# More projection beside the convolution's last stage, less beside its middle stages, and 256 bytes between two pools of a hybrid encoder layer

## The chip, the cores and the metric

The kernel runs on one core of a Trainium2 chip. The core has five engines with an instruction queue each: TensorE (PE, matrix products), VectorE (DVE), ScalarE (ACT), GpSimd (POOL) and SyncE (SP, which here only issues transfers). Transfers between DRAM and the on-chip memory (SBUF, 128 partitions) go through 16 DMA engines. Products land in PSUM, eight banks of 128 x 512 numbers. The metric is the device time of one execution in microseconds, lower is better; the median of three runs stands for a kernel.

## The reference

One layer of a bidirectional encoder on x of 2048 x 1024, all in float32:

```python
u = _rms_norm(h, norm_mix_g[l])
proj = u @ w_in[l]                                   # 1024 -> 3600 columns
hy = _short_conv_centred(proj[..., :HY_COLS], ...)   # 3 x 512 columns: z and two gates
spec = _hyena_filter_spectrum(L, ...)                # long filters, one per order and channel
y_hy = _group_rms_norm(_hyena(hy, spec, hy_skip[l]), hy_norm_g[l], HYENA_GROUPS)
qk = jax.nn.silu(_short_conv_centred(proj[..., HY_COLS:off], ...))
y_ml = _mlstm_bidirectional(q, k, v, o_pre, gates, ml_gate_b[l])
y_ml = _group_rms_norm(y_ml, ml_norm_g[l], MLSTM_HEADS)
h = h + concatenate([y_hy, y_ml]) @ w_out[l]
h = h + _cross_attention(_rms_norm(h, norm_x_g[l]), _rms_norm(mem, norm_mem_g[l]), wq, wk, wv, wo)
h = h + square(relu(_rms_norm(h, norm_ff_g[l]) @ ff_w1[l])) @ ff_w2[l]
return _rms_norm(h, final_norm_g)
```

`_hyena` does, for each of two orders, a convolution over the whole length by an FFT of twice the length, and a multiplication by a gate: `z = gate * (irfft(rfft(z) * spec[:, o]) + z * skip[o])`. `_mlstm_bidirectional` is a recurrence over chunks in both directions. The memory `mem` has 256 rows.

## The kernel before

Every large product is made of three products of operands split into a high and a low part (`mm3`, L353 to L359). The program is written by Python generators, each of which yields a stated cost before a piece of work; two generators are woven by these costs:

```python
def weave(a, b, wa, wb, until=False):
    ...
        if fb or (not fa and da / wa <= db / wb):
                da += next(a)
        else:
                db += next(b)
```

The weave fixes the program order. A planner then places the instructions on the engines' queues by a simulated timeline, with the program order as priority; instructions marked `keep_in_program_order` stay in order among themselves. At run time each queue is worked off in order.

The stretch in question weaves `rest` (the projections) with `p.hyena` (the long convolution) in the proportion 445 to 329 (L2125).

**Projections.** `sweep` (L748) makes transposed tiles, 128 columns by 512 rows, for the columns that need the short convolution; it yields 5.5 for 24 products and is heavy on DVE and ACT besides (short convolution, splits, transposes back). `natural` (L860) makes tiles of 128 rows by 256 columns for v and the gates; it yields 11 for four tiles and needs little of DVE and ACT. Beside them `gates` (L1076) and `states` (L1223, the backward recurrence) are stepped at fixed places. After the weave come the memory's projections `memproj` (L693: L708, L725, L737), with the first five steps of `mlstm` (L1227) between their steps.

**The convolution.** `hyena` (L905) has these stages: `spectrum` for order 0 (8 steps), then for each order 16 middle steps (loads of a block of the spectrum and of the filter, `response` L952, products L1030, element-wise complex product L1032 to L1036 on ACT, DVE and POOL, product back L987, store L989) and 8 last steps (load3, products L1048, gate L1051). For order 0 a last step goes on with `spectrum(1)`; for order 1 it takes squares on POOL (L1060), a sum (L1062), `bank_rsqrt` (L205 to L217) in a PSUM bank, L1064, two products on POOL (L1066) and the stores of `yh` (L1068). The yields that set its pace are 4.6 for a middle step, 6.0 for a last step of order 0 and 4.5 for one of order 1.

**PSUM.** The tags "mm" and "hy" have four banks each, given out in program order. The convolution, the recurrences and attention's transposes all use "hy".

**The mLSTM.** `mlstm` computes decay rows (L1275 to L1293), takes scores in a "hy" bank (L1284), and does 16 chunks one after the other (L1322 to L1356). Its pool `m_sb` lies on the space of the projections' x tiles.

**Attention.** `tail_open` (L1366) opens the pools of what comes next, on the left side of SBUF where the projections' and the convolution's pools were: `t_w` (first pair of weight tiles), `t_acc`, `t` (a pair of activation tiles and the second pair of weight tiles) and `t_n` (four staging tiles "wn" of 2 KB per partition, then two activation tiles). `mixed(0)` (L1484) loads the first four row blocks of `yh` into staging tiles (L1473), turns them on PE (L1479) and splits them; `gemm` then multiplies by the first and second pairs of w_out. Adding up the tiles, the pool `i_sb`, which the projections and `memproj` use (weights, memory tiles, small tiles), ends at byte 88,320 of a partition, and `t_n` begins at byte 88,064.

Of the kernel before, what the change touches and what calls it, by code (L numbers as in the profile page):

```python
# [10 lines left out]
F32 = mybir.dt.float32  # L11
# [117 lines left out]
class Prog:  # L129
# [775 lines left out]
    def hyena(self, es):  # L905
# [19 lines left out]
        def ta():  # L925
            return sb.tile([128, 2, CH], F32, tag="a", name="a", bufs=10)

        def tb():
            return sb.tile([128, CH], F32, tag="b", name="b", bufs=5)
# [12 lines left out]
        def load_filter(o, i):  # L942
            dm = sb.tile([128, 2, 128], F32, tag="dm", name="dm", bufs=3)
            nc.sync.dma_start(out=dm, in_=a["c_dm"][:, 2 * i:2 * i + 2])
            return dm, load_block(fs[o], i)

        def load2(o, i):
            em = sb.tile([128, 2, 128], F32, tag="em", name="em", bufs=2)
            nc.sync.dma_start(out=em, in_=a["c_em"][:, 2 * i:2 * i + 2])
            return em, load_block(sds[o], i)  # L950

        def response(i, dm, t):  # L952
            hr, hi = ta(), ta()
            for m in range(2):
                pp = self.mm()
                nc.tensor.matmul(pp, dm[:, m], t[:, m], start=True, stop=True)
                nc.scalar.copy(hr[0:64, m], pp[0:64])
                nc.scalar.copy(hr[64:128, m], pp[0:64])
                nc.vector.tensor_copy(hi[64:128, m], pp[64:128])
                nc.vector.tensor_copy(hi[0:64, m], pp[64:128])  # L960
                if i == 0 and m == 0:
                    nc.scalar.copy(hr[64:65, 0], pp[64:65])
                    for r in range(2):
                        nc.vector.memset(hi[64 * r:64 * r + 1, 0], 0.0)
            return dm, hr, hi

        def load3(o, j2):
            js = slice(2 * j2, 2 * j2 + 2)
            r = [ta() for h in range(2)]
            for h in range(2):  # L970
                self.by_phase(nc.sync, gds[o], j2, h, r[h], True)
            gate = ta()
            for q in range(4):
                nc.sync.dma_start(out=gate[phase[q]], in_=hy[1 + o, q, :, js])
            return r, gate
# [3 lines left out]
        def late(f):  # L979
            if held:  # L980
                held.pop()()
            if f is not None:
                held.append(f)

        def back(m, i, em, y, gs, dst):
            pg = self.hy()
            nc.tensor.matmul(pg, em[:, m], y, start=True, stop=True)  # L987
            nc.scalar.copy(gs[:, m], pg)
            nc.gpsimd.dma_start(out=of_block(dst, i, m), in_=gs[:, m])  # L989

        def spectrum(o, j2, z):
            st = [ta() for h in range(2)]
            pp = [self.hy() for q in range(4)]
            self.beside(*((pp[q][own[jj]], f1[phase[q]], z[phase[q], jj]) for q in range(4) for jj in range(2)),
                        pin=1 if o else 2)
            for i in range(2):
                for h in range(2):
                    (nc.vector.tensor_copy if h else nc.scalar.copy)(st[h][:, i], pp[2 * h + i])
            for h in range(2):
                self.by_phase(nc.gpsimd, sds[o], j2, h, st[h])  # L1000
# [12 lines left out]
        for o in range(2):  # L1013
            gd = gds[o]
            nxt = load2(o, 0)
            ready = response(0, *fq.pop(0))
            yield 4
            for i in range(16):
                yield 4.6
                dm, hr, hi = ready  # L1020
                em, t = nxt
                if i < 14:
                    fq.append(load_filter(o, i + 2))
                if i < 15:
                    nxt = load2(o, i + 1)
                    ready = response(i + 1, *fq.pop(0))
                gs = ta()
                for m in range(2):
                    pp = self.hy()
                    nc.tensor.matmul(pp, dm[:, m], t[:, m], start=True, stop=True)  # L1030
                    xt, y = tb(), tb()
                    nc.scalar.activation(xt[0:64], pp[64:128], AF.Copy, scale=-1.0)  # L1032
                    nc.scalar.copy(xt[64:128], pp[0:64])
                    nc.vector.tensor_tensor(y, pp, hr[:, m], ALU.mult)
                    nc.gpsimd.tensor_tensor(xt, xt, hi[:, m], ALU.mult)
                    nc.vector.tensor_tensor(y, y, xt, ALU.add)  # L1036
                    late(lambda m=m, i=i, em=em, y=y, gs=gs: back(m, i, em, y, gs, gd))
            late(None)
            nxt = load3(o, 0)
            yield 5  # L1040
            for j2 in range(8):
                yield 4.5 if o else 6.0
                js = slice(2 * j2, 2 * j2 + 2)
                r, gate = nxt
                if j2 < 7:
                    nxt = load3(o, j2 + 1)
                pp = [self.hy() for jj in range(2)]
                self.beside(*((pp[jj][phase[q]], e2[own[jj]], r[q // 2][own[jj], q % 2])  # L1048
                              for jj in range(2) for q in range(4)), pin=True)
                for jj in range(2):  # L1050
                    nc.vector.tensor_tensor(gate[:, jj], pp[jj], gate[:, jj], ALU.mult)  # L1051
                if o == 0:
                    late(lambda j2=j2, gate=gate: spectrum(1, j2, gate))
                    if j2 > 5:
                        fq.append(load_filter(1, j2 - 6))
                    continue
                y = gate.rearrange("q j (g e) -> q (j g) e", g=8)
                sq = ta()
                sqv = sq.rearrange("q j (g e) -> q (j g) e", g=8)
                nc.gpsimd.tensor_tensor(sqv, y, y, ALU.mult)  # L1060
                ms = sb.tile([128, 16], F32, tag="ms", name="ms", bufs=2)
                nc.vector.tensor_reduce(ms, sqv, AX.X, ALU.add)  # L1062
                rv = self.bank_rsqrt(sb, ms, 64)
                nc.vector.tensor_tensor(sqv, y, rv.unsqueeze(2).broadcast_to([128, 16, 64]), ALU.mult)  # L1064
                for jj in range(2):
                    nc.gpsimd.tensor_tensor(sq[:, jj], sq[:, jj], ghy, ALU.mult)  # L1066
                for q in range(4):
                    nc.gpsimd.dma_start(out=yh[q, :, js], in_=sq[phase[q]])  # L1068
            late(None)
# [296 lines left out]
    def tail_open(self, es):  # L1366
        def pool(name):
            return es.enter_context(self.tc.tile_pool(name=name, bufs=1))

        self.wp = [pool("t_w"), None]  # L1370
        for tag in ("wh", "wl"):
            self.wp[0].tile([128, 8, 256], F32R, tag=tag, name=tag)
        self.acc = pool("t_acc").tile([128, 8, 512], F32, name="acc")
        self.wp[1] = self.ap = pool("t")
        self.acts = 2
        for _ in range(2):
            self.act_tile("act")
        for tag in ("wh", "wl"):
            self.wp[1].tile([128, 8, 256], F32R, tag=tag, name=tag)
        self.T = pool("t_n")  # L1380
        self.acts = self.wps = 0

# [819 lines left out]
```

## Time and profile before

| | us |
|---|---|
| three runs | 3058.41, 3061.78, 3063.68 |
| median | 3061.78 |
| the profiled execution | 3063.97 |
| its span, first to last instruction | 3062.3 |

The span is the time from the first to the last instruction of the profiled execution; about 1.7 us lie around it. In the profile a line such as L1284 is a line of the listing above. PE is busy for 97% of the span and DVE for 64%. The mean clock granted to TensorE is 0.989 of full speed. Matmuls are pipelined: a product of 128 x 512 is shown for about 0.39 us, and the next begins 0.23 us after it.

The stages of the stretch, from the order of lines on PE:

| us from the span's start | what PE does |
|---|---|
| 351 to 410 | sweeps; the convolution's `spectrum` for order 0 |
| 408 to 620 | sweeps, then natural tiles; middle steps of order 0 |
| 638 to 735 | natural tiles, sweeps; last steps of order 0 |
| 745 to 955 | sweeps, natural tiles; middle steps of order 1 |
| 966 to 1087 | the last projections, then `memproj` from 997; last steps of order 1 |
| 1104 to 1132 | `memproj`; the first two chunks of the mLSTM |
| 1132 to 1172 | mLSTM chunks and attention's first turns, alone |
| from 1172 | attention woven with the rest of the mLSTM |

### The profile page before, as it was taken

Reading aid. Unit: us, or ns where it says so; the run is one execution under the profiler, and the core shown is the slowest. Engines: PE = TensorE matmul, PEld = TensorE weight load, DVE = VectorE, ACT = ScalarE, POOL = GpSimd, SP = SyncE. Lnnn points to the kernel's source line nnn. Section 1 sums busy time; section 2 is a strip of 40 time slices with the busy share of each in tenths; the row PEclk is TensorE's granted clock in tenths of the full one; section 3 lists DMA queues with packets and bytes.
Section 4 is the critical chain, followed back from the end, with each engine's and each line's share of the span. In section 5 each row is a group of like instructions: output and inputs, shape, how many; then the busy total and the mean of one; then the engine's idle time right before and its main releaser. Section 6 shows DMA issues by size and latency. Waiting matters only on the chain.

```text
span 3062.3 us, 44144 instructions
## 1 busy us (share of the span) xinstructions
PE 2979.0 (97%) x14799; PEld 2367.6 (77%) x14799; DVE 1953.2 (64%) x3442; ACT 1491.5 (49%) x2930; POOL 1263.4 (41%) x1025
## 2 busy tenths in 40 slices
PE   9999999998999989999999999999999999999998
PEld 7666667775678867888888888888888888888876
DVE  8855464557755447867665666558555686566695
ACT  6443455634664235555544455556555543333335
POOL 0112113321443654333223247765665374344653
PEclk9999999999999999999999999999999999999999
DMA  6655676686877976463567466657544555444434
GB/s 223 197 186 170 213 263 214 192 273 216 279 229 221 348 265 198 149 228 125 196 202 264 137 219 217 208 178 250 190 151 152 196 192 169 118 157 121 155 103 165
DMA packets 423644, 607.03 MB, mean 198 GB/s; under 512 B 36847, under 2 KB 229999, under 8 KB 422393
## 3 DMA queue, kind: packets, MB, share of 16 engines
q1 hardware_dynamic: 395972, 525.42, 53.6%
q0 software_dynamic: 18992, 62.96, 5.6%
q10 hardware_dynamic: 8452, 15.83, 1.4%
q8 instruction: 117, 1.92, 0.3%
q14 instruction: 111, 0.90, 0.1%
HBM read 401.67 MB, written 202.41 MB: 197 GB/s over the span
## 4 chain that ended last, share of the span: by engine, by line
PE 58%; DVE 2%; DMA 1%; issue 1%; ACT 1%; POOL 0%; SPq 0%; DVEq 0%; POOLq 0%; ACTq 0%
PE mm L355 12%; PE mm L359 12%; PE mm L358 12%; PE hy L355 6%; PE hy L359 6%; PE hy L358 6%; PE hy L1322 1%; PE hy L1324 1%; DVE bl L1693 0%; PE hy L1284 0%; PE hy L1596 0%; DVE acc L1991 0%; PE hy L1200 0%; PE hy L1479 0%; DVE acc L2028 0%
## 5 line engine op out<-in xcount | busy, mean ns | idle before, releaser
L1692 ACT CAST ah<-w 128x512 fp32r<-128x512 f32 x284 | 176.6, 623 | 303.8 <-PE hy L358 150.2
L1693 DVE TENSOR_TENSOR bl<-wr,bh 128x512 fp32r<-128x512 f32 x213 | 240.3, 1132 | 126.5 <-ACT bh L1692 126.2
L366 DVE TENSOR_TENSOR wl<-wn,wh 128x512 fp32r<-128x512 f32 (+1 forms) x296 | 220.0, 787 | 89.2 <-ACT wh L366 89.2
L355 PE MATMUL mm<-xh,wh 128*128 128x512 f32 x640 | 264.5, 415 | 2.3 <-ACT xh L366 1.1
L358 PE MATMUL mm<-xl,wh 128*128 128x512 f32 x640 | 255.9, 400 | 5.5 <-DVE xl L366 5.4
L359 PE MATMUL mm<-xh,wl 128*128 128x512 f32 x640 | 254.5, 398 | 0.0
L1692 ACT CAST bh<-wr 128x512 fp32r<-128x512 f32 x232 | 143.4, 621 | 227.9 <-PE mm L359 169.5
L1693 DVE TENSOR_TENSOR al<-w,ah 128x512 fp32r<-128x512 f32 x236 | 216.5, 918 | 57.2 <-ACT ah L1692 56.9
L359 PE MATMUL mm<-bh,al 128*128 128x512 f32 x576 | 223.8, 391 | 3.4 <-DVE al L1693 3.4
L355 PE MATMUL mm<-bh,ah 128*128 128x512 f32 x576 | 225.9, 392 | 1.3 <-DVE acc L1854 1.1
L358 PE MATMUL mm<-bl,ah 128*128 128x512 f32 x576 | 224.9, 390 | 0.0
L366 ACT CAST wh<-wn 128x512 fp32r<-128x512 f32 (+1 forms) x296 | 164.3, 620 | 102.6 <-PE mm L359 51.1
L358 PE MATMUL mm<-act,wh 128*128 128x512 f32 x512 | 202.0, 395 | 0.0
L359 PE MATMUL mm<-act,wl 128*128 128x512 f32 x512 | 199.9, 392 | 0.0
L355 PE MATMUL mm<-act,wh 128*128 128x512 f32 x512 | 199.0, 395 | 0.6 <-ACT wh L366 0.5
L355 PE MATMUL hy<-bh,ah 128*128 128x512 f32 x448 | 175.2, 391 | 0.0
L358 PE MATMUL hy<-bl,ah 128*128 128x512 f32 x448 | 174.6, 390 | 0.0
L359 PE MATMUL hy<-bh,al 128*128 128x512 f32 x448 | 174.4, 390 | 0.0
L331 POOL TENSOR_TENSOR b<-b 128x512 f32<-128x512 f32 x32 | 48.1, 1504 | 293.6 <-DVE b L330 277.4
L355 PEld LDWEIGHTS mm<-xh,wh 128*128 128x128 f32 x640 | 121.1, 190 | 52.4 <-issue 18.7
L358 PEld LDWEIGHTS mm<-xl,wh 128*128 128x128 f32 x640 | 121.2, 189 | 50.9 <-issue 19.1
L355 PE MATMUL mm<-wh,xh 128*128 128x256 f32 (+1 forms) x512 | 155.7, 304 | 1.8 <-DVE a L960 1.8
(396 smaller groups left out, 8257.4 us busy)
## 6 DMA issues: line engine op xcount, KB each, us to landing
wr<-hc SPq DMA_DIRECT2D x224, 256.0 KB
w<-in_ff_w_dram SPq DMA_DIRECT2D x172, 256.0 KB
hc<-wn SPq DMA_DIRECT2D x128, 256.0 KB
wn<-in_w_in_dram SPq DMA_DIRECT2D x100, 256.0 KB
hc<-q SPq DMA_DIRECT2D x96, 256.0 KB
fs<-a SPq DMA_DIRECT2D x32, 512.0 KB
zs<-a POOLq DMA_DIRECT2D x32, 512.0 KB, 6.6
a<-fs SPq DMA_DIRECT2D x64, 256.0 KB
```

What stands on the lines that cost most here:

```text
L331: nc.gpsimd.tensor_tensor(b, f, b, ALU.subtract)
L355: first = mm(ps, lh, rh, start=start, stop=False)
L358: mm(ps, lh, rl, start=False, stop=False)
L359: self.last = mm(ps, ll, rh, start=False, stop=stop)
L366: both = (self.nc.scalar.copy(hi, src), self.nc.vector.tensor_tensor(lo, src, hi.bitcast(F32), ALU.subtract))
L1322: nc.tensor.matmul(dst, nm[:, h], va[:, h], start=True, stop=state is None)
L1324: nc.tensor.matmul(dst, rows_[d, 1][:, h], state[:, h], start=False, stop=True)
L1692: self.nc.scalar.copy(hi, src)
L1693: eng.tensor_tensor(lo, src, hi.bitcast(F32), ALU.subtract)
```

## The change

Two yields in `hyena` and one more pool in `tail_open`. The middle steps of both orders state a cost of 3.7 in place of 4.6. The last steps of order 1 state 8.0 in place of 4.5; those of order 0 keep 6.0. A pool of one unused tile of 64 numbers (256 bytes per partition) is opened ahead of `t_n`, so that `t_n`, and with it everything opened later on that side, begins at byte 88,320 in place of 88,064. No instruction is added or removed by the text; the order in which the planner places them is made anew.

```diff
             for i in range(16):
-                yield 4.6
+                yield 3.7
                 dm, hr, hi = ready
...
             for j2 in range(8):
-                yield 4.5 if o else 6.0
+                yield 8.0 if o else 6.0
                 js = slice(2 * j2, 2 * j2 + 2)
...
         for tag in ("wh", "wl"):
             self.wp[1].tile([128, 8, 256], F32R, tag=tag, name=tag)
+        pool("t_even").tile([128, 64], F32, name="t_even")
         self.T = pool("t_n")
```

## The prediction

> **What bounds the kernel now.** I read the page first, then busy time by stage, then what TensorE (PE) waited for in the stages where it was not full.
>
> ```profile
> span 3062.3 us, 44144 instructions
> PE 2979.0 (97%) x14799; PEld 2367.6 (77%) x14799; DVE 1953.2 (64%) x3442; ACT 1491.5 (49%) x2930; POOL 1263.4 (41%) x1025
> ```
>
> PE is busy for 2979.0 of 3062.3 us. The change removes no product, so it can only win or lose in the 83 us of PE idle time, and in the half-speed clock that follows idle time. The windows cut the stretch that the change touches at the convolution's stages: middle stage of order 0, its last stage, middle stage of order 1, its last stage (955 to 1104, in three pieces), and what follows.
>
> ```profile
> core 0: us, PE busy (x) PEld busy (x) DVE busy (x) ACT busy (x) POOL busy (x), PEclk, DMA share, GB/s
> 410.00:640.00 230.00, 223.62 (x1249) 169.17 (x1248) 139.22 (x219) 140.19 (x248) 78.07 (x85) 0.99 0.69 216
> 640.00:735.00 95.00, 84.19 (x548) 57.08 (x554) 55.03 (x169) 31.67 (x53) 9.52 (x17) 0.96 0.82 261
> 735.00:955.00 220.00, 212.57 (x1020) 151.69 (x1006) 144.47 (x249) 135.48 (x236) 87.78 (x97) 1.00 0.73 227
> 955.00:997.00 42.00, 42.00 (x304) 37.21 (x304) 22.20 (x48) 13.84 (x20) 15.56 (x17) 1.00 0.97 303
> 997.00:1050.00 53.00, 50.64 (x266) 42.06 (x273) 23.60 (x77) 17.22 (x43) 36.15 (x44) 0.97 1.04 350
> 1050.00:1104.00 54.00, 54.00 (x262) 37.95 (x247) 24.27 (x68) 12.06 (x23) 33.84 (x39) 1.00 0.98 341
> 1104.00:1132.00 28.00, 28.00 (x145) 19.86 (x144) 13.72 (x38) 14.63 (x50) 16.59 (x19) 1.00 0.69 217
> 1132.00:1172.00 40.00, 23.89 (x139) 21.77 (x138) 27.16 (x101) 22.51 (x86) 18.73 (x18) 0.74 0.59 186
> ```
>
> The last row is the worst: PE is idle for 16.1 of 40 us there, with a granted clock of 0.74. Its waits (engine and line, what it waited for: us, times, longest) are those of a serial chain:
>
> ```profile
> PE hy L1322 <- DVE bry L213: 5.1, 1, 5.1
> PE hy L1479 <- DVE act L366: 5.0, 1, 5.0
> PE hy L1200 <- ACT ht L1336: 2.5, 2, 2.1
> PE hy L1284 <- issue: 1.6, 1, 1.6
> ```
>
> L1284 to L1336 is the mLSTM; L1479 turns attention's first rows of y. Why does the chain stand alone? First and last start of a few lines tell (durations min/median/max, then the starts; L1060 over its first four steps, then over all eight):
>
> ```profile
> L708 PE MATMUL mm<-mt,wm x256: 377/379/483, 997.1 to 1109.6; 128*128 128x256 f32 x128
> L737 PE MATMUL mm<-wm,kt x64: 592/592/595, 1079.2 to 1131.1; 128*128 128x512 f32 x64
> L1293 ACT ACTIVATE rw<-rw,cols x16: 385/386/402, 1001.3 to 1005.7; 128x128 f32<-128x128 f32 x16
> L1284 PE MATMUL hy<-qn,kk_t x48: 272/275/421, 1104.1 to 1169.1; 128*128 128x128 f32 x48
> L1060 POOL TENSOR_TENSOR a<-a x4: 1885/1887/1888, 971.8 to 1035.5; 128x1024 f32<-128x1024 f32 x4
> L1060 POOL TENSOR_TENSOR a<-a x8: 1883/1888/1904, 971.8 to 1093.3; 128x1024 f32<-128x1024 f32 x8
> L1064 DVE TENSOR_TENSOR a<-a,hy x8: 1220/1220/1221, 980.8 to 1101.5; 128x1024 f32<-128x1024 f32 x8
> ```
>
> The memory's products begin with L708 at 997 and end with L737 at about 1131.5 us. The mLSTM's first decay rows were ready at 1006 (L1293), but its first scores (L1284) ran at 1104.1, 1.4 us after the convolution's last L1064 ended (1101.5 + 1.2). The code gives the reason: `scores` takes the next "hy" PSUM bank, and these four banks go round in program order behind the convolution's last `bank_rsqrt`. So the convolution's slow last stage holds the mLSTM back by some 98 us, and of the four chunks written beside the memory's products two run after them with nothing large beside. That is the stall at 1132.
>
> **The change part by part.** The pacer advances projections by 445 for each 329 of the convolution's stated costs. Projection costs are near microseconds: 24 products of 128x512 make 5.5, and 14 steps in this stretch take 52.87 - 49.69 = 3.18 us, 0.227 each, so 24 take 5.45.
>
> ```profile
> 49.69 0.40 PE L355 MATMUL mm<-xh,wh 128*128 128x512 f32 x1
> ...
> 52.87 0.39 PE L359 MATMUL mm<-xh,wl 128*128 128x512 f32 x1
> ```
>
> *Middle steps, 4.6 to 3.7:* each of 32 loses 0.9 x 445/329 = 1.22 us of projection beside it, 39 us in all. *Last steps of order 1, 4.5 to 8.0:* each of 8 gains 4.7 us, 38 us in all. The convolution's total goes from 334.8 to 334.0, so both still run out of cost together; only the last stage begins earlier. Counting the yields, its first step is written when 374 of 451 projection units are out, not 407: 33 us earlier, at about 933 us where it is now 966 (the first L1060 at 939 where it is 971.8).
>
> How fast will its steps go? The rows of L1060 give 63.7 / 3 = 21.2 us a step at first, 57.8 / 4 = 14.5 us for the last four, 17.4 over all. The slow ones lie where the DMA engines are full (shares 0.97 and 1.04), since the memory's weights come in beside the step's own transfers. Begun 33 us earlier, most of the steps precede those weights. At 14.5 the last L1064 starts at 980.8 - 33 + 7 x 14.5 = 1049; at today's 17.2 (120.7 / 7) at 1069. I take 1060: the mLSTM starts about 41 us earlier than now. Another thing it needs, the backward states, had left the core for DRAM by the row below (last store at 1047.4), so they don't hold it later than that.
>
> ```profile
> L1219 POOL DMA_DIRECT2D cbd<-cb x9: 560/580/610, 922.4 to 1047.4; - x9
> ```
>
> 41 us covers the 40 us stretch. What is it worth? 16.1 us of idle time, and the half-speed clock: in the two low pieces below PE is busy for 8.74 + 4.28 = 13.0 us at half, which is 6.5 us lost. At most 22.6 us.
>
> ```profile
> 1140.20:1153.90 13.70, 8.74 (x37) 8.17 (x38) 10.60 (x41) 6.24 (x26) 7.31 (x7) 0.50 0.41 134
> 1164.10:1171.00 6.90, 4.28 (x21) 4.28 (x21) 6.26 (x21) 4.05 (x9) 0.00 (x0) 0.51 0.55 176
> 1020.80:1024.20 3.40, 3.40 (x8) 2.73 (x9) 1.40 (x2) 1.61 (x4) 3.40 (x4) 0.50 1.03 416
> ```
>
> *The 256-byte tile `t_even`:* it adds no instruction. The addresses of the program before put the end of the projections' and the memory's pool at byte 88,320 of a partition, and the staging pool `t_n` at 88,064; its first tile overlaps by 256 bytes. A pool's space is free only when all of its tiles are, and the trace shows that: the queue waited for the memory's last product.
>
> ```profile
> SPq L1473 <- PE mm L737: 1.6, 1, 1.6
> 1131.77 0.81 SPq L1473 DMA_DIRECT2D wn<-yh  x2
> ```
>
> After the change these four loads need only the convolution's end, so they, the 16 turns and the 24 products on the first pair of weights (5.5 us) can stand ready when L737 ends. Queued behind them on SP are the mLSTM's kn, qn and kk_t, which then also stop waiting for L737. What is late next is the second pair of weights, still in the memory's space: nothing if the 5.5 us cover its split, 5 us (the present wait for act) if not. Of the 22.6 us I take 18; bounds 0 and 22.6.
>
> *The stall in the memory's first keys* (row below) and the 3.4 us at half clock behind it are worth 2.4 + 1.7 = 4.1 us. It falls where DMA is full; I take 2, bounds 0 and 4.
>
> ```profile
> PE mm L725 <- ACT kt L710: 2.4, 1, 2.4
> ```
>
> [...]
>
> *The middle stages' lost cover.* Per step PE, DVE and ACT are now busy 212.57, 144.47 and 135.48 / 16 = 13.3, 9.0 and 8.5 us; with 1.2 us less of PE work they still are at 75% or less. Idle time there is 7.4 us, of which:
>
> ```profile
> PE hy L1030 <- DMA a<-zs: 3.2, 1, 3.2
> PE mm L355 <- DVE a L960: 1.8, 1, 1.8
> PE hy L987 <- DVE b L1036: 1.6, 2, 1.3
> ```
>
> The first is the change of order, once. The other 4.2 us lie beside seven steps with transposed projections (sweeps), which load DVE and ACT; by the yields there will be 13 such steps. Six more at 0.6 us cost 3.6; I take 4, bounds 0 and 39 (all the cover lost). The 10.8 us of idle time in 640 to 735 keep their cause (the round trip between orders, and the gates' chain beside it); the gates move to the middle steps of order 1. I take 0, bounds 8 either way, two thirds of what is idle there.
>
> Sum: -18 - 2 + 4 = -16 us. The profiled execution took 3063.97 us, 2.2 above the median; from the median 3061.78 the sum gives **3046 us**.
>
> **The rivals.** *Its own chain paces the last stage.* If all its steps go at 21.2 us, as the first do, the last L1064 starts at 948 + 148 = 1096, 5 us earlier than now, and the stall stays but for that: with the middle stages' 4 us, 3061. The same follows if the planner, which places instructions by its own simulated times, does not put the stage earlier: it lags its written place already (all of it is written ahead of L708, which begins at 997, and it ends at 1103). Against it: the steps speed up as soon as the back states end, and DMA is at 0.73 where the first steps will now lie.
>
> *Slower: the middle stages' latency.* If a middle step cannot go faster than now, because its loads, its DVE and its POOL work follow one another, the 39 us of cover return as PE idle time: 3062 - 20 + 39 = 3081. It decides from 20 us on, 0.6 us for each of 32 steps, half of what is taken away. Against it: PE is 97% busy there, so PE paces the steps now, and their idle time is 13.8 us for 32 steps. For it: the 4.2 us above lie beside the sweeps, and more of the steps are to lie there.
>
> **How the numbers follow.** Forecast 0.60 (own range 3036 to 3056), chain or planner 0.26 (3055 to 3067), slower 0.14 (3064 to 3081). A measurement of this kernel can tell about 0.2%, 6 us, from no change: 3055.7 to 3067.9. Faster: 0.57 of the first and 0.05 of the second, 0.62. Same: 0.03, 0.20 and 0.03, so 0.26. Slower 0.12. The range is 3032 to 3069: it takes in the first two cases, and leaves out 0.1 above and less below (every bound at its best, -35 us, is not to be had at once).
>
> **What would show it.** Right: the last L1060 near 1050, the first L1284 near 1060, loads wn<-yh issued before L737 ends, and the 40 us behind L737 with PE full and the clock at 1. In the middle stages idle time stays below 20 us. Wrong: L1284 still behind 1090; or waits for L1036, L960 or a<-zs that grow; or L1479 and L355 waiting after L737 for the second pair's split.

## The result and the profile after

| | us |
|---|---|
| kernel before, median of 11 runs (lowest to highest) | 3062.72 (3058.41 to 3067.0) |
| kernel after, median of 11 runs (lowest to highest) | 3070.66 (3065.26 to 3074.77) |
| time after / time before | 1.0022, 95% interval 1.0013 to 1.003 |
| the profiled execution after, its span | 3069.03, 3067.3 |

The change makes the kernel slower by 0.22%; 3046 was forecast. The span and the busy times of the page after:

```profile
span 3067.3 us, 44143 instructions
PE 2984.0 (97%) x14799; PEld 2361.9 (77%) x14799; DVE 1944.3 (63%) x3442; ACT 1491.6 (49%) x2930; POOL 1260.5 (41%) x1025
```

TensorE's idle time is the same as before (3067.3 - 2984.0 = 83.3 us, before 3062.3 - 2979.0 = 83.3). It has only moved, as the windows by stage show. First the kernel before, then the one after; the rows are: order 0's middle steps, the change of order (its last steps up to order 1's first middle step), order 1's middle steps, the stretch up to the memory's first product (L708), and 186 us from there, which hold the memory's products and the seam to attention.

```profile
core 0: us, PE busy (x) PEld busy (x) DVE busy (x) ACT busy (x) POOL busy (x), PEclk, DMA share, GB/s
415.00:615.00 200.00, 193.62 (x1024) 143.25 (x1023) 113.61 (x181) 124.17 (x222) 69.29 (x76) 0.98 0.67 211
615.00:754.00 139.00, 124.98 (x810) 90.32 (x810) 89.20 (x229) 55.23 (x97) 22.84 (x32) 0.98 0.82 258
754.00:945.00 191.00, 186.78 (x897) 133.22 (x897) 123.56 (x208) 117.62 (x204) 80.08 (x87) 1.00 0.74 230
945.00:997.00 52.00, 52.00 (x351) 45.00 (x350) 30.35 (x61) 20.88 (x31) 18.19 (x21) 1.00 0.84 261
997.00:1183.00 186.00, 167.53 (x862) 131.22 (x862) 95.86 (x308) 70.63 (x216) 111.60 (x125) 0.94 0.85 284
```

```profile
413.00:597.00 184.00, 173.75 (x848) 121.36 (x847) 108.80 (x168) 117.67 (x209) 67.69 (x76) 0.98 0.71 222
597.00:733.00 136.00, 122.09 (x857) 89.45 (x856) 71.85 (x141) 50.18 (x89) 20.72 (x31) 0.92 0.81 254
733.00:923.00 190.00, 177.56 (x727) 117.03 (x726) 136.94 (x281) 119.66 (x205) 68.11 (x76) 0.96 0.71 213
923.00:1030.00 107.00, 105.33 (x711) 89.72 (x710) 55.85 (x142) 31.37 (x52) 46.79 (x50) 1.00 0.81 248
1030.00:1216.00 186.00, 181.81 (x963) 146.51 (x962) 102.88 (x301) 88.45 (x268) 108.90 (x117) 1.00 0.84 284
```

The last row is the gain: idle time falls from 18.5 to 4.2 us and the clock is full. The second and third rows are the price: in order 1's middle steps idle time rises from 4.2 to 12.4 us, and the granted clock falls to 0.92 at the change of order and to 0.96 behind it. I count as **lost** the idle time of a stretch and half of the time that its clock records show at 0.50 (in the kernel after, products of 128 x 256 begin 0.21 us apart at 0.50, from 883.4 to 886.2, and 0.12 us apart behind it, at full clock):

| lost us | order 0's middle | change of order | order 1's middle | to L708 | memory and seam | sum |
|---|---|---|---|---|---|---|
| before | 9.8 | 17.4 | 4.2 | 0.0 | 30.4 | 61.8 |
| after | 13.7 | 24.0 | 19.4 | 1.7 | 4.2 | 63.0 |

So 26.2 us were won at the seam and 27.4 lost ahead of it. The count serves for large differences only: the span less this sum lies between 2996.9 and 3007.8 us over all the kernels of this study, so it doesn't resolve the last few us (here it shows 1.2 of the 5.0 us between the two spans). It also counts idle time inside a half-clock piece twice. Counted once, as the prediction did at the seam (idle time, and half of PE's busy time at 0.50), 22.5 us were won at the seam (26.7 to 4.2) and 23.9 lost ahead of it (30.9 to 54.8): 4.0, 3.4, 14.8 and 1.7 us by stage. Over the whole spans this second count gives 105.7 and 106.1 us; so 4.6 of the 5.0 us between the two profiled executions lie in neither idle time nor half clock, and where they lie isn't shown.

What TensorE waited for between 410 and 1030 in the kernel after (the six largest; line, what it waited for: us, times, longest):

```profile
PE hy L1030 <- DMA a<-zs: 6.8, 2, 3.9
PE mm L956 <- issue: 5.3, 2, 3.0
PE hy L173 <- DMA a<-zg: 4.4, 2, 2.7
PE mm L956 <- DMA a<-fs: 3.7, 2, 3.4
PE hy L173 <- ACT a L998: 3.0, 1, 3.0
PE mm L956 <- DVE a L960: 2.3, 2, 1.2
```

Three of them are loads from DRAM: of zs and zg, which the stage ahead has stored there, and of fs, the filters' response, stored before this stretch. They come to 14.9 us in all. In the kernel before it was 6.9 us: 3.2 for zs, which the prediction shows, and

```profile
PE hy L173 <- DMA a<-zg: 2.6, 1, 2.6
PE mm L956 <- DMA a<-fs: 1.1, 1, 1.1
```

The starts that the prediction had named (in kernels with `t_even`, lines from 1380 on stand one higher than in the listing), and the issue of the loads of y:

```profile
L1284 PE MATMUL hy<-qn,kk_t x128: 270/275/377, 1093.9 to 1458.8; 128*128 128x128 f32 x128
L737 PE MATMUL mm<-wm,kt x64: 592/592/595, 1117.1 to 1174.0; 128*128 128x512 f32 x64
L708 PE MATMUL mm<-mt,wm x256: 377/379/381, 1030.3 to 1158.8; 128*128 128x256 f32 x128
L1060 POOL TENSOR_TENSOR a<-a x8: 1884/1906/1914, 948.0 to 1087.8; 128x1024 f32<-128x1024 f32 x8
```

```profile
1105.20 1.80 SPq L1474 DMA_DIRECT2D wn<-yh  x4
```

The mLSTM's first scores (L1284) came 10.2 us earlier than before, not 41. But the memory's products were pushed back: L708 begins 33 us later and L737 ends with its last start at 1174.0 in place of 1131.1. The first scores now lie 80 us ahead of the last L737, where it was 27 us, and the loads of y are issued 69 us ahead of it. Both dates, that of the scores and that of the memory's products, come after the time lost ahead of L708: 27.4 us more than before by the count, which is most of L708's 33 us (an estimate) and delays the scores as well. In e4b_last below, which loses about as much ahead as the kernel before (29.9 and 31.4 us), the scores come 31.6 us earlier and L737 ends 12.5 us later. The stall is gone by both moves: the scores come earlier in the work, and the memory's products later.

### The profile page after: what moved, and what is told of

The parts are those of the page before. It is cut to its first block, busy times and chain, and to the rows that moved or that the text cites. A ratio compares the mean times of both kernels' runs of the same rounds, so it can differ in the third digit from the quotient of the medians.

```text
span 3067.3 us, 44143 instructions
## 1 busy us (share of the span) xinstructions
PE 2984.0 (97%) x14799; PEld 2361.9 (77%) x14799; DVE 1944.3 (63%) x3442; ACT 1491.6 (49%) x2930; POOL 1260.5 (41%) x1025
## 4 chain that ended last, share of the span: by engine, by line
PE 80%; DMA 6%; DVE 6%; issue 4%; ACT 2%; POOL 1%; SPq 1%; DVEq 0%; POOLq 0%; ACTq 0%
PE mm L355 17%; PE mm L358 16%; PE mm L359 16%; PE hy L355 6%; PE hy L359 6%; PE hy L358 6%; PE hy L173 2%; PE mm L956 1%; PE mm L708 1%; PE hy L1030 1%; PE hy L987 1%; DMA a<-zg 1%; PE hy L1322 1%; PE hy L1324 1%; PE mm L725 1%
## 5 line engine op out<-in xcount | busy, mean ns | idle before, releaser
L355 PE MATMUL mm<-xh,wh 128*128 128x512 f32 x640 | 265.6, 417 | 4.2 <-ACT st L201 1.4
L355 PE MATMUL mm<-bh,ah 128*128 128x512 f32 x576 | 225.9, 392 | 0.1
L355 PE MATMUL mm<-act,wh 128*128 128x512 f32 x512 | 199.5, 395 | 0.8 <-ACT wh L366 0.8
L355 PE MATMUL hy<-bh,ah 128*128 128x512 f32 x448 | 175.2, 391 | 0.0
L355 PEld LDWEIGHTS mm<-xh,wh 128*128 128x128 f32 x640 | 120.8, 189 | 56.3 <-issue 21.7
L355 PE MATMUL mm<-wh,xh 128*128 128x256 f32 (+1 forms) x512 | 155.0, 303 | 0.8 <-DVE a L960 0.4
```

The costliest lines, as they stand in the source:

```text
L355: first = mm(ps, lh, rh, start=start, stop=False)
```

## The experiments

Theory A at the start: the middle stages' lost cover costs about as much as the seam wins. Its rivals: t_even made the gain (B); any new order of the program moves the time by as much (C); the wide last steps, 8.0, make the loss (D). Every run is a ratio to the kernel before, taken on the same chip in the same set of runs.

### One part at a time

`e1_even` has t_even alone; `e2_yields` the two yields alone; `e3_mid` the 3.7 and t_even; `e4_last` the 8.0 and t_even.

```diff
# e3_mid, against the kernel after
-                yield 8.0 if o else 6.0
+                yield 4.5 if o else 6.0
# e4_last, against the kernel after
-                yield 3.7
+                yield 4.6
```

> The kernel before with t_even alone (yields 4.6 and 4.5). Theory A (less cover in the middle stages costs some 25 us, the early last stage with t_even wins some 22): the loads wn<-yh no longer wait for L737, but the mLSTM chain still stands alone behind L737, since its scores still wait for the last stage's banks; only the 5.0 us of L1479 <- act go: 3058 (3055 to 3062). Theory B (t_even alone made the gain at the seam): 3041 to 3046. Theory C (any rearrangement moves the planner's order by some 8 us, whatever it is): anywhere from 3054 to 3071.

> The kernel after without t_even (yields 3.7 and 8.0). Theory A: the middle stages stay as in the kernel after (3070.7); behind L737 the loads wn<-yh wait again for L737, then 16 turns and a split, but chunks of the mLSTM are later in the program beside them: 3 to 8 us of idle time return at the seam: 3075 (3072 to 3079). Theory B: without t_even nothing of the gain of some 22 us is left: 3090. If t_even is worth nothing: 3070.

> Middle steps 3.7, last steps of order 1 kept at 4.5, with t_even. The middle steps are written as in the kernel after, the last stage begins as early, and its steps stand closer. Theory A: the middle stages' loss of some 25 us is there, with the a<-zs and half-clock pieces at 419, and the gain at the seam too: 3070 (3064 to 3074). Rival D (the loss comes from the last stage's 8.0, its steps spread too far): 3045 to 3052.

> Last steps of order 1 at 8.0, middle steps kept at 4.6, with t_even. Everything to about 960 is written as in the kernel before; the projections run out after four last steps, the other four stand alone in the program ahead of the memory's products. Theory A: middle stages as before (PE idle near 25 us in 410 to 997), the seam as before or a little better: 3059 (3054 to 3066). Rival D (8.0 itself costs): 3070 or more.

| run | ratio (95%) | median us | lost ahead of L708 | lost at memory and seam |
|---|---|---|---|---|
| e1_even | 1.0005 (0.9993 to 1.0017) | 3063.15 | 26.5 | 28.7 |
| e2_yields | 1.004 (1.0025 to 1.0055) | 3071.54 | 56.9 | 9.8 |
| e3_mid | 1.005 (1.0035 to 1.0065) | 3075.15 | 60.0 | 12.3 |
| e4_last | 0.9948 (0.9932 to 0.9965) | 3043.55 | 37.7 | 8.5 |

The last steps at 8.0, with t_even, make the kernel 0.5% *faster*, which I had not expected: theory A had 3059 for it. The middle steps at 3.7, with t_even, make it 0.5% slower. Each of the two edits takes most of the stall at the seam away by itself (30.4 us before; 8.5 and 12.3), and only the middle steps bring the large loss ahead of L708 (31.4 before; 37.7 and 60.0). Rivals B and D fall; of rival C more is said below, where effects add up that a mere reshuffling would scatter.

t_even alone does nothing that can be told from zero. TensorE's two largest waits between 1100 and 1170 in e1_even, and its loads of y:

```profile
PE hy L1322 <- DVE bry L213: 5.1, 1, 5.1
PE hy L1480 <- DVE act L366: 4.8, 1, 4.8
```

```profile
1105.17 1.76 SPq L1474 DMA_DIRECT2D wn<-yh  x4
```

The loads run ahead, at 1105 and not at 1131.77, as the prediction said. But the wait for the split `act` is as long as before (5.0), so it never hung on the loads.

To see what 8.0 does, `e4_last` was run again as `e4b_last`, with its twin without t_even, `e7_last_noeven`.

> The kernel with the last steps alone at 8.0 (middle steps 4.6, t_even) once more, as the measure for the three others of this set: 3044 (3040 to 3048).

> The same without t_even: last steps of order 1 at 8.0 and nothing else of the change. If t_even is what lets attention's first loads run ahead of L737: the loads wait for L737 again and 5 to 6 us come back, as between the kernel after and the one without t_even: 3049 (3046 to 3053). If the seam is gone for another reason (the mLSTM's first chunks lie beside the memory's products): 3044.

Measured: 0.9945 (0.9933 to 0.9958) and 0.9963 (0.9952 to 0.9975), 3041.78 and 3049.24 us. Both as expected: once the chain's stall is gone, the loads of y are late next, and t_even is worth 5.5 us (0.18%); between the kernels after and e2_yields the difference is the same 0.18%. Each of the two is uncertain by nearly as much as it is large; they agree, and the traces below show the wait. The stages of e4b_last (same five windows), and three lines of it:

```profile
413.00:611.00 198.00, 192.79 (x1027) 142.43 (x1026) 113.98 (x181) 124.50 (x222) 69.68 (x76) 0.99 0.67 213
611.00:747.00 136.00, 122.56 (x800) 87.61 (x800) 87.62 (x227) 54.87 (x97) 22.49 (x32) 0.97 0.81 260
747.00:938.00 191.00, 188.04 (x905) 134.53 (x904) 122.77 (x210) 117.78 (x204) 80.01 (x87) 1.00 0.74 233
938.00:999.00 61.00, 57.79 (x392) 48.58 (x391) 35.33 (x87) 20.86 (x32) 26.98 (x32) 1.00 0.86 268
999.00:1185.00 186.00, 180.35 (x958) 142.91 (x957) 108.67 (x321) 85.48 (x259) 113.73 (x121) 0.99 0.87 301
```

```profile
L1284 PE MATMUL hy<-qn,kk_t x128: 270/275/377, 1072.5 to 1430.4; 128*128 128x128 f32 x128
L737 PE MATMUL mm<-wm,kt x64: 592/592/594, 1081.7 to 1143.6; 128*128 128x512 f32 x64
L1060 POOL TENSOR_TENSOR a<-a x8: 1887/1890/1904, 965.0 to 1062.2; 128x1024 f32<-128x1024 f32 x8
```

The middle stages are as before. By the count of yields the projections run out after four of the eight last steps, and the steps take 13.9 us each (97.2 / 7; 17.4 before). With their products ahead of the memory's, L737 ends 12.5 us later than before and the scores start 31.6 us earlier, 71 us ahead of the last L737. The kernel without t_even, by the same views:

```profile
1151.75 1.81 SPq L1473 DMA_DIRECT2D wn<-yh  x4
```

```profile
L737 PE MATMUL mm<-wm,kt x64: 592/592/594, 1092.5 to 1151.1; 128*128 128x512 f32 x64
```

```profile
PE hy L1479 <- DMA wn<-yh: 3.8, 3, 3.0
```

Here the loads go out 0.65 us behind the start of the last L737, and the turns wait for them.

### Which order's steps, and is it DVE?

`e5_o0` and `e6_o1` shorten the middle steps of one order only, with last steps at 8.0 and t_even. `e8_dve` and `e9_dve_last` take DVE work away beside order 1's middle steps, from the kernel after and from e4_last: they leave out two of the three taps of the short convolution for three column blocks, 12 instructions of about 1.3 us.

```diff
# e5_o0 (e6_o1 the other way round), against the kernel after
-                yield 3.7
+                yield 3.7 if o == 0 else 4.6
# e8_dve, against the kernel after, and e9_dve_last, against e4_last
-                        nc.vector.scalar_tensor_tensor(v, P[:, use:use + n], cw[:, 0, ct:ct + 1], v, ALU.mult, ALU.add)
-                        nc.vector.scalar_tensor_tensor(v, P[:, use + 2:use + 2 + n], cw[:, 2, ct:ct + 1], v, ALU.mult, ALU.add)
+                        if first or c2 not in (5, 8, 9):
+                            nc.vector.scalar_tensor_tensor(v, P[:, use:use + n], cw[:, 0, ct:ct + 1], v, ALU.mult, ALU.add)
+                            nc.vector.scalar_tensor_tensor(v, P[:, use + 2:use + 2 + n], cw[:, 2, ct:ct + 1], v, ALU.mult, ALU.add)
```

> Only order 0's middle steps at 3.7, order 1's at 4.6, last steps of order 1 at 8.0, with t_even: one half of what separates the kernel with the last steps alone at 8.0 (3043.6) from the kernel after (3070.7), 27 us. By stage the traces put some 7 us of it at order 0's first middle step (3.9 idle behind a<-zs and 6.8 at half clock), 6 to 7 at the change of order, and 13 beside the sweeps in order 1. Theory A1 (the loss is where short steps lie beside the sweeps and the gates, which load DVE): mostly order 1's, so here 3050 to 3054. Rival A2 (every step that loses cover loses alike): 3057. Rival A3 (it is the place at which the projections then stand when order 1 begins that counts, not the steps' length): 3062 or more.

> Only order 1's middle steps at 3.7, order 0's at 4.6, last steps of order 1 at 8.0, with t_even. Theory A1: 3056 to 3062. Rival A2: 3057. Rival A3: 3043 to 3050, as order 1 then begins where it did in the kernel before.

> The kernel after with the two taps of the short convolution (L798, L799) left out in the second pass of columns 5, 8 and 9, which lie beside order 1's middle steps: 12 instructions of 1.28 us, 15 us less on DVE; the output is wrong for these columns. If DVE's load beside short steps is what PE waits for there (A1): idle time and half clock in 735 to 900 fall by 8 us or more, 3056 to 3062. If it is the loads and the round trip of the step itself (A2): 3067 to 3071.

> The kernel with the last steps alone at 8.0 (middle steps 4.6, t_even), with the same two taps left out in the same columns, as the measure of what this leaving out is worth where the cover is whole: by both theories 3040 to 3044, since PE waits for DVE only 2 to 4 us there.

| run | ratio (95%) | median us | lost: order 0's middle, change of order, order 1's middle |
|---|---|---|---|
| e5_o0 | 1.0003 (0.9991 to 1.0014) | 3059.89 | 13.6, 25.4, 6.2 |
| e6_o1 | 0.9972 (0.9961 to 0.9982) | 3051.01 | 9.5, 21.3, 6.9 |
| e8_dve | 1.0007 (0.9996 to 1.0018) | 3061.62 | 15.4, 23.3, 11.4 |
| e9_dve_last | 0.9929 (0.9909 to 0.9948) | 3038.67 | 9.7, 16.4, 4.0 |
| e4b_last, for comparison | 0.9945 (0.9933 to 0.9958) | 3041.78 | 6.9, 16.8, 3.0 |

Against e4b_last, order 0's short steps cost 0.58% and order 1's 0.27%: the other way round than theory A1 (DVE beside the sweeps) had it. Leaving 15 us of DVE work out is worth 0.15% in the kernel after and 0.16% where the cover is whole: the same, though each figure is uncertain by 0.15 to 0.23% (e9_dve_last ran four times). The 3061.62 of e8_dve lies at the end of A1's range, but its twin gains as much where no cover is missing. The trace of e8_dve does lose 8 us less in order 1's middle steps than that of the kernel after (a second profile of the latter, e17_after below, has 14.5 there, 3 us more), but the times don't follow. So A1 is not borne out, and not excluded for a few us. A3, that it matters where the projections stand when order 1 begins, came nearest.

### Place or length

Order 0's short steps have a second effect. Theory E says that the loss hangs on the place at which order 1 begins, theory F that it hangs on the steps' length. Counting the yields, order 1's first middle step is written behind 302.5 units of projections in the kernel before, and behind 280.5 in the kernel after, since nothing gave the 16 x 0.9 = 14.4 back to order 0. These runs tell the place from the length:

```diff
# e10_place, against e4_last: order 0's steps short, the place kept
-                yield 4.6
+                yield 4.6 if o else 3.7
-                yield 8.0 if o else 6.0
+                yield 8.0 if o else 7.8
# e14_back, against the kernel after: the place put back, nothing else
-                yield 8.0 if o else 6.0
+                yield 8.0 if o else 7.8
# e15_early, against e4_last: the place moved, the steps as before
-                yield 8.0 if o else 6.0
+                yield 8.0 if o else 4.2
# e16_lump, against the kernel after: the place put back ahead of the last steps
-            yield 5
+            yield 5 if o else 19.4
```

> Order 0's middle steps at 3.7, its last steps at 7.8 in place of 6.0, order 1 as in the kernel before in its middle steps (4.6), last steps 8.0, with t_even: the 14.4 units taken from order 0's middle steps are given to its last steps, so that the change of order is written at the same projection as in the kernel before (302.5 units), and not 22 units earlier. Theory E (the round trips through DRAM at the changes of stage lose their cover when the change of order moves ahead of the natural tiles' end and beside the gates; the steps' length in itself costs little): only the first wait for a<-zs at 419 stays, 3050 (3046 to 3053). Theory F (order 0's short steps themselves lose, wherever the change of order is): as with order 0's middle steps alone at 3.7, 3058 (3055 to 3063).

> The kernel after (middle steps 3.7 in both orders, last steps of order 1 at 8.0, t_even) with order 0's last steps at 7.8 in place of 6.0 and nothing else: the change of order is written at 302.5 projection units, as in the kernel before, not at 280.5. Theory E (the place of the change of order carries the loss): 3049 (3044 to 3054), of the kernel after's 27 us some 20 gone. Theory F (short steps lose wherever it is): 3062 or more.

> Middle steps 4.6 in both orders as before, last steps of order 1 at 8.0, t_even, but order 0's last steps at 4.2 in place of 6.0: the change of order is written at 280.5 units, as in the kernel after, with the steps' old length. Theory E: 3056 to 3064, 15 us or more above the kernel with the last steps alone at 8.0 (3042); idle time and half clock at the change of order rise. Theory F: 3042 to 3047.

> The kernel after with the yield behind order 0's first load3 at 19.4 in place of 5 and nothing else: the change of order is written at 302.5 units again, but the 14.4 units stand in one lump ahead of order 0's last steps, whose own yields stay 6.0. If the place carries the 13 us: 3055 (3051 to 3059), as with the steps at 7.8. If it is the cover beside order 0's last steps: 3068 (3065 to 3072), as the kernel after.

> The kernel after once more: 3069 (3066 to 3072), 0.22 to 0.3 per cent above the kernel before.

| run | middle steps | order 1 begins at | ratio (95%) | median us |
|---|---|---|---|---|
| e4_last, e4b_last | 4.6 | 302.5 | 0.9948, 0.9945 | 3043.55, 3041.78 |
| e10_place | 3.7 and 4.6 | 302.5 | 0.9944 (0.9932 to 0.9957) | 3041.69 |
| e14_back | 3.7 | 302.5 | 0.9979 (0.997 to 0.9988) | 3054.89 |
| e16_lump | 3.7 | 302.5 | 0.9982 (0.9972 to 0.9992) | 3054.91 |
| e15_early | 4.6 | 280.5 | 0.9988 (0.9977 to 1.0) | 3056.12 |
| after, e17_after | 3.7 | 280.5 | 1.0022, 1.0019 (1.0007 to 1.0031) | 3070.66, 3067.94 |

This is a table of two causes, and they add up (each ratio is uncertain by about 0.001, a difference by 0.0015). The **place** costs 0.0042 with long steps (0.9988 - 0.9946) and 0.004 with short ones (1.002 - 0.998), some 12 to 13 us. The **length** costs 0.0034 at the old place (0.998 - 0.9946) and 0.0032 at the new one (1.002 - 0.9988), some 10 us, nearly all of it order 1's, since order 0's short steps cost nothing in e10_place, where its last steps get what the middle ones lose. e16_lump leaves order 0's last steps as they are and gives what e14_back gives: it is the place, not the cover beside these steps. Theory E alone had 3049 for e14_back, F alone 3062 or more; both have a part. For e10_place both had more than came (3050 and 3058, measured 3041.69).

One thing goes along with both causes: every later stage moves too. By the same count order 1's last stage is written behind 412.5 units in e4_last and e10_place, 390.5 in e14_back, e16_lump and e15_early, and 374 in the kernel after. No run changes the place alone, or order 1's length alone, and leaves the last stage where it was, so "place" and "length" hold what that move costs; and by the last stage's place alone the six rows would fall in line too (0.9946, then 0.998 to 0.9988, then 1.002). Against that stand e5_o0 and e6_o1, both with 390.5 and 0.0031 apart, and the traces: the change of order loses 23 to 36 us in all kernels that write it at 280.5, and 11 to 21 us in those that write it at 302.5; order 1's middle steps lose 7 to 19 us in all kernels with 3.7 there, and 3 to 6 us with 4.6 and the starts' yields as before.

The change of order and order 1's middle steps behind it, in e15_early and then in e16_lump:

```profile
616.00:737.00 121.00, 101.41 (x668) 67.05 (x667) 64.58 (x126) 42.59 (x76) 19.86 (x30) 0.86 0.84 271
737.00:927.00 190.00, 187.55 (x882) 132.72 (x881) 136.68 (x289) 123.83 (x214) 76.77 (x84) 1.00 0.73 225
```

```profile
601.00:757.00 156.00, 146.10 (x983) 109.62 (x982) 94.44 (x242) 62.10 (x110) 21.83 (x33) 0.97 0.77 240
757.00:926.00 169.00, 163.29 (x755) 112.40 (x754) 114.37 (x187) 112.22 (x193) 73.07 (x81) 0.98 0.77 237
```

e15_early loses 19.6 us idle and 14% of the clock at the change of order and next to nothing behind it; e16_lump, with steps that are shorter, loses 9.9 us and 3%. What the place does in detail (which product of the neighbouring sweeps or gates is in the way) was not tried and stays open.

### More cover at the starts

PE's waits at the starts of the middle stages (a<-zs) looked like the plain remedy: more projections ahead of the first step.

```diff
# e11_trips, against e4_last
-            yield 4
+            yield 8
-            yield 5
+            yield 8
# e12_start, against e4_last: middle steps 4.35, so that the stages keep their places
-            yield 4
+            yield 8
# e13_mix: as e12_start, order 0's middle steps 3.6 and its last steps 7.5
```

> Middle steps 4.6, last steps of order 1 at 8.0, t_even, and more cover at the changes of stage: the yield ahead of an order's first middle step is 8 in place of 4, that behind its first load3 is 8 in place of 5 (4 to 5 us of projections more beside each round trip). Theory E: PE's waits for a<-zs, a<-zg and a<-fs in 410 to 1030 fall from 6.9 us to 3 or less, with some half clock behind them: 3038 (3034 to 3042). If the round trips are longer than the cover or PE's program order, not the cover, sets these waits: 3042 to 3047.

> More cover at the start of the middle stages, with every later stage at its place: the yield ahead of an order's first middle step 8 in place of 4, middle steps 4.35 in place of 4.6 (16 x 0.25 = 4), last steps of order 1 at 8.0, t_even. Theory E: the waits for a<-zs at the starts go (3.5 us and the half clock behind), as in the run in which both starts got 4 more, but the last stage stays: 3036 (3032 to 3041). If the place alone counts and cover nothing: 3042.

> As the one before, and order 0's last steps at 7.5 in place of 6.0, paid for by its middle steps at 3.6 (beside natural tiles for the most part); order 1's middle steps 4.35; the change of order at its old place. Theory E: 3033 (3029 to 3040), the lowest of all. Theory F: 3047 or more, as order 0's steps are shorter than in the kernel after.

| run | ratio (95%) | median us | lost: order 0's middle, change of order, order 1's middle, to L708, memory and seam |
|---|---|---|---|
| e11_trips | 1.0024 (1.0013 to 1.0036) | 3067.17 | 2.4, 23.2, 12.9, 5.2, 26.7 |
| e12_start | 0.9971 (0.996 to 0.9981) | 3051.77 | 2.3, 17.8, 12.2, 6.8, 11.1 |
| e13_mix | 0.9999 (0.999 to 1.0008) | 3058.53 | 11.6, 13.3, 13.0, 8.8, 9.3 |

All three came out worse than e4b_last. The local effect is there: in e11_trips and e12_start no wait for a<-zs is left, and order 0's middle steps lose 2.4 and 2.3 us where e4b_last lost 6.9. But e11_trips writes the last stage 19 units later (14 x 445 / 329), its first L1060 runs at 1003.3 and not at 965.0, the scores start only 39 us ahead of the last L737, and the old stall at the seam is back (26.7). e12_start keeps the places in the count and still has other waits further on. The three largest at its change of order:

```profile
PE hy L1134 <- ACT cv L796: 4.1, 1, 4.1
PE hy L173 <- DVE a L998: 3.1, 1, 3.1
PE hy L173 <- DMA a<-zg: 2.4, 1, 2.4
```

Now the gates' chain (L1134) and the convolution's own last steps are the largest, and a load (zg) is still the third. Why order 1's middle steps lose 12 to 13 us in these runs stays open. Of the versions that compute the whole layer, none beat e4_last and e10_place, which are level at 0.9945 and 0.9944, 17 us faster than the kernel before.

## Why the prediction was wrong

**What bounds the kernel: right.** PE stayed at 97%, and the large gains and losses of the stages lie in its idle time and the half clock behind it.

**The seam: right in kind and nearly in size.** -18 there and -2 in the memory's first keys were taken; in the prediction's own count 22.5 us came, of 26.7 that were to be had. The place of it was read rightly (two chunks with nothing large beside them), but the step "the mLSTM starts about 41 us earlier than now" did not hold: it was 10.2, and the memory's products ended 42.9 us later. What is lost ahead delays both, and the prediction had 4 us for it; e4b_last, which loses no more there than the kernel before, has 31.6 and 12.5. The distance that counts, from the first scores to the last L737, grew by 53 us in the kernel after and by 44 in e4b_last. The first steps of the last stage (L1060) began at 948.0 in place of 971.8, and took 20.0 us each (to 1087.8), not 14.5 to 17.2: "its own chain paces the last stage" had that nearly right. It didn't decide the time: over the runs the seam's loss goes with how far the scores start ahead of the last L737.

| | before | e1_even | e11_trips | e3_mid | e4b_last | e2_yields | after |
|---|---|---|---|---|---|---|---|
| first L1284 ahead of last L737, us | 27 | 27 | 39 | 61 | 71 | 77 | 80 |
| lost at memory and seam, us | 30.4 | 28.7 | 26.7 | 12.3 | 7.4 | 9.8 | 4.2 |

**t_even: right in what it frees, wrong in what hung on it.** With the stall there it was worth nothing, and the wait for `act` stayed; with the stall gone it is worth 5.5 us, by the loads' wait.

**The failed step: "The middle stages' lost cover ... I take 4", and "I take 0" for the change of order.** The trace has 3.9 in order 0's middle, 6.6 at the change of order, 15.2 in order 1's middle and 1.7 up to L708, 27.4 us in all, or 23.9 with idle time counted once; the runs put 23 us on it (1.002 - 0.9946). Two things went wrong. The mean over a step (PE 13.3, DVE 9.0, ACT 8.5 us) was read as slack that each step has, and where the waits would grow was looked for inside the steps. And the prediction saw that the last stage moves ahead of projections but priced only the gain of it; that the change of order moves too, by 22 units, was mentioned ("the gates move to the middle steps of order 1") and put at 0. That place, with what moves behind it, was worth 12 to 13 us. Half of the 27.4 us is idle time ahead of L708 (38.3 us, up from 24.6); the other half is half clock, which the prediction had priced at the seam and not here.

**The rival "slower: the middle stages' latency"** has the right sign and not the right mechanism. It said that a step can't go faster than now. Order 0's did: the starts of L1030 run from 423.1 to 594.7 where they ran from 424.7 to 613.4, 17 us less. e10_place shows that this costs nothing when the place is kept. Order 1's did not in the kernel after, where it looks as the rival said: 196.2 us (724.6 to 920.8) after 197.7 (745.8 to 943.5). But with the same 3.7 and the old place they did: 176.3 us in e14_back and 174.0 in e6_o1. So the step's own latency alone does not hold them there; what lies beside them differs with the place, and which part of it holds them was not tried. Of its 39 us, order 1's steps gave some 10.

**What would show it** was well chosen in part: L1284 behind 1090 and growing waits for a<-zs were named as signs that the forecast is wrong, and both came; idle time in the middle stages was 22.7 us, not below 20. Full PE behind L737 was named as a sign that it is right, and came too: the two were taken for one question.

**The half clock.** The 3.4 us at half clock behind the keys' wait of 2.4 us, which the prediction priced at 1.7 us, don't stand alone: the kernel after has half clock behind waits of 1.8 to 3.9 us, see the last section.

## What to carry to other kernels

An edit of stated costs in a woven program moves every later stage along the other strand: count where each stage change is written before and after, and give back ahead of the change what was taken, or price the move as a change of its own. When a stall is taken away by one edit, look which of the change's parts does it alone; here the last steps' yield with t_even gave a gain of 0.55% alone, and the shorter middle steps on top of it only added the loss. And cover is not made at a start for nothing: in the three runs that tried it, it was taken out of the stages behind or moved them, and more came back there as other waits.

## What the runs showed of the hardware

**Half clock followed waits of 1.8 to 3.9 us, and not each time.** Two stretches at half clock of the kernel after (the first begins within the last us of the 3.9 us wait for a<-zs; the second 1.2 us behind the start of the 3.0 us wait for L998, with the 3.4 us for a<-fs inside it):

```profile
422.30:429.00 6.70, 5.94 (x8) 2.75 (x9) 2.08 (x3) 3.72 (x7) 1.26 (x1) 0.50 0.84 261
695.40:705.50 10.10, 4.88 (x21) 1.60 (x21) 5.41 (x12) 1.75 (x3) 1.06 (x2) 0.50 0.91 301
```

One and the same wait, L956's for its issue at 462 us, is 2.9 us long in e5_o0, with the first of these rows behind it, and 3.0 us long in the kernel after, where the second row, from 461 to 472, has the full clock:

```profile
465.80:469.10 3.30, 3.30 (x7) 1.35 (x6) 3.23 (x6) 1.98 (x3) 1.83 (x2) 0.50 1.08 295
```

```profile
461.00:472.00 11.00, 8.03 (x39) 5.16 (x38) 7.67 (x11) 7.12 (x12) 4.86 (x5) 1.00 1.01 322
```

In the kernel after a wait of 1.8 us (L855's for a L960) ends at 882.4 us, one of 0.4 us (L355's for st L203) at 883.0, and half clock begins at 883.1:

```profile
883.10:886.40 3.30, 3.30 (x16) 3.30 (x17) 3.12 (x5) 1.22 (x4) 1.64 (x2) 0.50 1.11 301
```

In the traces of the kernels before and after, 20 stretches at half clock end ahead of the last instruction: 11 are 3.41 us long by the clock records, seven 6.83, one 10.24 and one 13.65 us. Why one and the same wait has half clock behind it in one kernel and not in another was not shown.

**The spread of one kernel goes with the granted clock.** The 12 runs of e1_even lie between 3051.85 us (mean clock 0.992) and 3070.7 us (0.989): 19 us, more than most of the effects that were sought. The difference of these clocks is worth some 9 us of it (an estimate, 0.003 x 3061); the rest stays open. A single profile of such a kernel tells where the time goes, not how much it is: e4_last's own profiled run (3051.63) was its slowest.
